# The gathered token tile has its experts picked first, and its rows are asked for while the dense tiles are still being picked

## Chip, cores and metric

The kernel runs on one core of one Trainium2 chip. The metric is device time in microseconds of one execution. TensorE is called PE, VectorE DVE, ScalarE ACT, GpSimd POOL, and SyncE, which issues most of the DMAs, SP.

## What is computed

Two transformer blocks over 512 tokens of width 1024, in f32. The change lies in the second half of the first block, a layer of 16384 small experts. Each token scores 8 heads against two sets of 128 keys, takes the 16 best of each set, then the 16 best of their sums: 128 experts a token, with a softmax gate each.

```python
def peer_sublayer(h, g_ffn, w_peer_q, keys_1, keys_2, peer_u, peer_v):
    x = rmsnorm(h, g_ffn).reshape(-1, shape[-1])
    q = (x @ w_peer_q).reshape(T, PEER_HEADS, PEER_DQ)
    s1 = jnp.einsum('thd,kd->thk', q[..., :half], keys_1).astype(jnp.float32)
    s2 = jnp.einsum('thd,kd->thk', q[..., half:], keys_2).astype(jnp.float32)
    v1, i1 = lax.top_k(s1, PEER_TOPK)
    v2, i2 = lax.top_k(s2, PEER_TOPK)
    cand = (v1[..., :, None] + v2[..., None, :]).reshape(T, PEER_HEADS, PEER_TOPK * PEER_TOPK)
    sc, ci = lax.top_k(cand, PEER_TOPK)
    ...
    act = jax.nn.gelu(jnp.einsum('td,tkd->tk', xt, peer_u[it]), approximate=False)
    return jnp.einsum('tk,tkd->td', gt * act, peer_v[it])
```

## The kernel before

The 512 tokens are four tiles of 128. Tiles 0, 1 and 2 are *dense*: they are multiplied with all 16384 experts, 128 blocks of 128, and a table of gates, zero for experts not picked, keeps what counts. Tile 3 (`GT`) is *gathered*: each token fetches its own 128 rows of `peer_u` and of `peer_v`, in 256 indirect DMAs of 128 rows by 1024 f32 (512 KB), issued by POOL.

**A front** (`front(e)`) loads block e of u (512 KB, by SP), splits it into a high and a low half (`wh` on ACT, `wl` on POOL or, in the loop, on DVE), does 24 matmuls for the dense tiles, and writes the Gelu of the result into a tile `act`. **A product** (`gated_acts`, `products`) loads block e of v, splits it, multiplies `act` by the gates (`gin`, a DMA of 1.5 MB for 8 blocks), splits that into `ah` and `al`, and adds 18 matmuls into six banks `py`.

**Picking.** `topkeys(t)` finds the best keys of tile t on DVE (L914 to L918); `topk(t)` the best sums, and the expert indices through one-hot tiles, compared on DVE (L1051), multiplied on POOL (L1055) and summed on DVE (L1057). For a dense tile indices and gates are transposed into `eT` (L1069); for `GT` they stay in `eg` and `gg`. `spread(t)` makes the gate table of a dense tile in 32 steps: DVE compares (L1080), ACT or POOL scales four one-hots by the gates (L1086, L1083), PE multiplies them, ACT copies the result (L1090), and after four steps SP writes 1 MB to `gates`. `beside(a, na, b, nb)` interleaves two such sequences; each piece calls `step()`, which puts in a front whenever the count of fronts times `PACE` falls behind the steps plus `LEAD`. So 64 of the 128 fronts come before the loop. In this stage a scheduler chooses each engine's order from what is ready.

**The loop** runs over 126 blocks: a product each, and the other 64 fronts spread evenly. POOL and DVE go there in the order of the code. A gather (L960) fills one of four tiles `row`; DVE multiplies it with the token's `xg` and sums (L965, u) or adds it to `yg` (L975, v), two gathers behind the issue. Gathers start at iteration 10 and end at the last. Behind the loop come two last blocks, the sums of each tile and the second transformer block.

**Memory.** The `act` tiles live in two pools, even blocks in one and odd blocks up to `EARLY` in the other. Fronts 42 to 63 (`HOLD` to `AHEAD`) are written to DRAM (`ahead`) and fetched back by `back(e + 5)`.

The functions that the change touches:

Of the kernel before, what the change touches and what calls it, by code (L numbers as in the profile page):

```python
# [26 lines left out]
GT = 3  # L27
# [139 lines left out]
def build(tc, A, OUT):  # L167
# [753 lines left out]
    HOLD, AHEAD = 42, 64  # L921
    ad = dp.tile([AHEAD - HOLD, P, TD], F32, name="ahead")
    EARLY = 84
# [5 lines left out]
    def act_tile(e, side):  # L929
        return (tr if side else tp).tile([P, TD], F32, name="act", bufs=21 if side else 24)  # L930
# [27 lines left out]
    def gather(src, k):  # L958
        r = tg.tile([P, D], F32, name="row", bufs=4)
        G.indirect_dma_start(out=r, out_offset=None, in_=src,  # L960
                             in_offset=bass.IndirectOffsetOnAxis(ap=eg[:, k:k + 1], axis=0))
        return r
# [109 lines left out]
    def spread(t):  # L1072
        NPL = (0, 0, 2)[t]

        t0, eT = t * P, picks[t]
        for b0 in range(0, P, TB):
            stg = tn.tile([P, P, TB], F32, name="stg", bufs=2)
            for q0 in range(0, TB, 4):
                a1 = tn.tile([P, 2, 4, P], F32, name="oh12", bufs=4)
                V.tensor_tensor(a1, iota[:, None, None, :].to_broadcast([P, 2, 4, P]),  # L1080
                                eT[:, :2, b0 + q0:b0 + q0 + 4, None].to_broadcast([P, 2, 4, P]), op=OP.is_equal)
                for q in range(NPL):
                    G.tensor_tensor(a1[:, 1, q], a1[:, 1, q], eT[:, 2, b0 + q0 + q:b0 + q0 + q + 1].to_broadcast([P, P]),  # L1083
                                    op=OP.mult)
                for q in range(NPL, 4):
                    S.activation(a1[:, 1, q], a1[:, 1, q], AF.Copy, scale=eT[:, 2, b0 + q0 + q:b0 + q0 + q + 1])  # L1086
                ps = mmps()
                for q in range(4):
                    TE.matmul(ps[:, q * P:(q + 1) * P], a1[:, 1, q], a1[:, 0, q], start=True, stop=True)  # L1089
                S.copy(stg[:, :, q0:q0 + 4], ps.rearrange("p (q e) -> p e q", q=4))  # L1090
                yield
            nc.sync.dma_start(gd[:, :, (t0 + b0) // TB].rearrange("g p x -> p g x"),
                              stg.rearrange("p (g e) t -> p g (e t)", e=NE))
    order = (0, 1, 2, GT)
    for c in range(2):
        for j in range(2 - 2 * c, 4, 2):
            queries((4 * c + j, 4 * c + j + 1), [w_pq(4 * c + j), w_pq(4 * c + j + 1)])
        for _ in topkeys(0, range(4 * c, 4 * c + 4)):
            pass
# [5 lines left out]
    PACE, LEAD = 3.6, 10  # L1105
    steps = [0]

    def step():

        steps[0] += 1  # L1110
        while len(done_u) < AHEAD and len(done_u) * PACE < steps[0] + LEAD:
            front(len(done_u))
# [12 lines left out]

    beside(topk(0), 23, topkeys(1, range(8)), 16)
    for t in range(3):
        beside(spread(t), 32, chain(topk(t + 1), topkeys(t + 2, range(8)) if t < 2 else iter(())), 39 if t < 2 else 40)
    todo = [("u_rows", g_u, k) for k in range(128)] + [("v_rows", g_v, k) for k in range(128)]
    rows = []  # L1130
    LAG = 2
# [32 lines left out]
    ngather, G0 = len(todo), 10  # L1164
    def use_row():
        f, k, r = rows.pop(0)
        f(k, r)

    with tc.manual_schedule(engines={mybir.EngineType.Pool, mybir.EngineType.DVE}):
        parts, u = gated_acts(0), u_of(AHEAD)  # L1170
        for e in range(P - 2):
# [5 lines left out]
            back(e + 5)  # L1177
# [4 lines left out]
            while len(todo) > max(0, min(ngather, (P - 3 - e) * ngather // (P - 2 - G0))):  # L1182
                src, f, k = todo.pop(0)
                if len(rows) == LAG:
                    use_row()
                if src == "v_rows" and k == 0:
                    while rows:
                        use_row()
                rows.append((f, k, gather(A[src], k)))
# [3 lines left out]
            if e == EARLY + 16:  # L1193
# [440 lines left out]
```

## Time and profile before

| | |
|---|---|
| time, median of 3 runs (lowest, highest) | 2778.35 us (2774.49, 2782.89) |
| the profiled execution: its own time, its span | 2781.33 us, 2779.3 us |
| PE busy | 2621.9 us, 94% |
| DVE busy | 1712.1 us, 62% |
| ACT busy | 1134.9 us, 41% |
| POOL busy | 1039.6 us, 37% |
| DMA, mean over the span | 165 GB/s |

Busy shares are means over stages with different limits. Picking lies between about 625 and 1046 us of the span and the expert loop between 1061 and 1873; what the change is worth is read there.

### The profile page before, as it was taken

The numbers are of one execution on the slowest core, as the hardware profiler recorded it, in microseconds if no ns is written. First come the engines' busy times: TensorE is split into PE (matmuls) and PEld (weight loads), VectorE is DVE, ScalarE is ACT, GpSimd is POOL, SyncE is SP. The second block draws the span as 40 slices with busy tenths as digits, with TensorE's granted clock in tenths as the row PEclk, the third lists the DMA queues.
The fourth block names the chain that finished last, engine by engine and source line by source line (L and its number), as shares of the span: only waits on it lengthen the run. The fifth ranks groups of instructions, "written<-read, shape, count | busy, mean of one in ns | idle before, by whom it ended". The sixth has DMA issues, their size and how long they took to land.

```text
span 2779.3 us, 37248 instructions
## 1 busy us (share of the span) xinstructions
PE 2621.9 (94%) x13809; PEld 2244.2 (81%) x13809; DVE 1712.1 (62%) x3398; ACT 1134.9 (41%) x2064; POOL 1039.6 (37%) x767
## 2 busy tenths in 40 slices
PE   7889999998899898999999999998999999999997
PEld 6768878798899887888888787887666687878886
DVE  5673342248797863788888887896699522533333
ACT  4463342243676553333333333333566432422322
POOL 2322122326546690354455454452333233211111
PEclk9999999999999999999999999998999999999998
DMA  2312213323354566799999889893210133222221
GB/s 100 114 54 78 71 65 125 117 80 101 118 162 150 169 195 238 270 337 360 350 357 345 313 319 339 309 321 136 72 36 24 43 99 98 107 83 99 91 97 55
DMA packets 172485, 458.33 MB, mean 165 GB/s; under 512 B 15248, under 2 KB 73488, under 8 KB 165648
## 3 DMA queue, kind: packets, MB, share of 16 engines
q1 hardware_dynamic: 131984, 316.97, 32.7%
q0 software_dynamic: 36864, 134.23, 14.0%
q10 hardware_dynamic: 3456, 4.76, 0.7%
q8 instruction: 108, 1.77, 0.3%
q14 instruction: 73, 0.60, 0.1%
HBM read 417.43 MB, written 33.69 MB: 162 GB/s over the span
## 4 chain that ended last, share of the span: by engine, by line
PE 60%; DVE 11%; issue 10%; POOL 8%; DMA 3%; ACT 3%; ACTq 0%; SPq 0%; POOLq 0%; DVEq 0%
PE mm L249 33%; PE pu L249 10%; PE py L1161 8%; POOL row L960 4%; PE mm L1089 2%; POOL oh L1055 2%; PE tp L1487 1%; PE o L1492 1%; DVE s L1475 1%; DMA wr<-in_u_T_dram 1%; DVE yg L975 1%; DVE vl L211 1%; POOL wl L211 1%; DVE oh L1080 1%; DMA row<-in_v_rows_dram,eg 1%
## 5 line engine op out<-in xcount | busy, mean ns | idle before, releaser
L211 POOL TENSOR_TENSOR wl<-wr,wh 128x1024 fp32r<-128x1024 f32 (+3 forms) x135 | 325.0, 2408 | 532.8 <-ACT wh L210 237.8
L210 ACT CAST wh<-wr 128x1024 fp32r<-128x1024 f32 (+2 forms) x271 | 274.3, 1012 | 408.3 <-PE mm L249 218.2
L249 PE MATMUL pu<-xf,wh 128*128 128x384 f32 x2048 | 392.2, 343 | 6.8 <-ACT act L947 6.8
L249 PEld LDWEIGHTS pu<-xf,wh 128*128 128x128 f32 x2048 | 362.3, 191 | 13.1 <-ACT act L947 7.8
L960 POOL DMA_INDIRECT row<-in_u_rows_dram,eg x128 | 185.8, 1452 | 263.2 <-DVE row L965 238.6
L960 POOL DMA_INDIRECT row<-in_v_rows_dram,eg x128 | 191.5, 1496 | 190.8 <-DVE yg L975 167.5
L1161 PE MATMUL py<-vh,ah 128*128 128x512 f32 x768 | 202.8, 399 | 29.9 <-ACT ah L210 29.8
L211 DVE TENSOR_TENSOR wl<-wr,wh 128x1024 fp32r<-128x1024 f32 (+2 forms) x136 | 160.5, 1180 | 102.8 <-PE mm L249 61.3
L249 PE MATMUL pu<-xf,wl 128*128 128x384 f32 x1024 | 203.7, 341 | 15.3 <-POOL wl L211 15.3
L1161 PE MATMUL py<-vl,ah 128*128 128x512 f32 x768 | 201.5, 398 | 0.0
L249 PEld LDWEIGHTS pu<-xf,wl 128*128 128x128 f32 x1024 | 183.4, 191 | 18.8 <-POOL wl L211 18.7
L1161 PE MATMUL py<-vh,al 128*128 128x512 f32 x768 | 197.3, 392 | 0.0
L1161 PEld LDWEIGHTS py<-vh,ah 128*128 128x128 f32 x768 | 144.9, 192 | 60.8 <-ACT ah L210 35.8
L210 ACT CAST ah<-act 128x384 fp32r<-128x384 f32 x128 | 65.6, 513 | 312.8 <-DVE act L1151 305.7
L211 DVE TENSOR_TENSOR vl<-vr,vh 128x1024 fp32r<-128x1024 f32 x128 | 156.2, 1221 | 49.3 <-ACT vh L210 49.2
L210 ACT CAST vh<-vr 128x1024 fp32r<-128x1024 f32 x128 | 134.5, 1051 | 125.0 <-PE py L1161 55.8
L1080 DVE TENSOR_TENSOR oh<-iota,eT 128x1024 f32<-128x1024 f32 x96 | 159.5, 1689 | 38.5 <-PE mm L1089 27.3
L975 DVE SCALAR_TENSOR_TENSOR yg<-row,ag,yg 128x1024 f32<-128x1024 f32 x127 | 162.8, 1282 | 19.5 <-DMA row<-in_v_rows_dram,eg 17.5
L1161 PEld LDWEIGHTS py<-vl,ah 128*128 128x128 f32 x768 | 148.4, 193 | 31.9
L1161 PEld LDWEIGHTS py<-vh,al 128*128 128x128 f32 x768 | 145.8, 190 | 30.7
L965 DVE SCALAR_TENSOR_TENSOR row<-row,xg 128x1024 f32<-128x1024 f32 x128 | 152.3, 1220 | 18.8 <-DMA row<-in_u_rows_dram,eg 18.6
L372 DVE TENSOR_TENSOR h<-mm,h 128x512 f32<-128x512 f32 (+1 forms) x54 | 34.1, 632 | 184.9 <-PE mm L249 184.9
(461 smaller groups left out, 5230.6 us busy)
## 6 DMA issues: line engine op xcount, KB each, us to landing
wr<-in_u_T_dram SPq DMA_DIRECT2D x128, 512.0 KB
vr<-in_v_rows_dram SPq DMA_DIRECT2D x128, 512.0 KB
wwr<-in_w_f_dram SPq DMA_DIRECT2D x32, 1024.0 KB
gates<-stg SPq DMA_DIRECT2D x24, 1024.0 KB
gin<-gates SPq DMA_DIRECT2D x16, 1536.0 KB
wr<-in_w_gm_dram SPq DMA_DIRECT2D x16, 512.0 KB
ahead<-act SPq DMA_DIRECT2D x22, 192.0 KB
act<-ahead SPq DMA_DIRECT2D x22, 192.0 KB
```

The costliest lines, as they stand in the source:

```text
L210: S.copy(hi, src)
L211: (lo_eng or V).tensor_tensor(lo, src, hi.bitcast(F32), op=OP.subtract)
L249: TE.matmul(out, w[a][k][:, c0:c0 + P], act[b][k][:, t0:t0 + n], start=i == 0 and k == 0, stop=i == 2 and k == kt - 1)
L372: V.tensor_tensor(h1[k][:, a:b], ps[:, a:b], h1[k][:, a:b], op=OP.add)
L960: G.indirect_dma_start(out=r, out_offset=None, in_=src, in_offset=bass.IndirectOffsetOnAxis(ap=eg[:, k:k + 1], axis=0))
L965: V.scalar_tensor_tensor(r, r, 1.0, xg, op0=OP.mult, op1=OP.mult, accum_out=ag[:, k:k + 1])
L975: V.scalar_tensor_tensor(yg[0], r, ag[:, k:k + 1], yg[0], op0=OP.mult, op1=OP.add)
L1055: G.tensor_tensor(ov[:, h], ov[:, h], iv[:, 4 * c + h, None].to_broadcast([P, 16, 16]), op=OP.mult)
L1080: V.tensor_tensor(a1, iota[:, None, None, :].to_broadcast([P, 2, 4, P]), eT[:, :2, b0 + q0:b0 + q0 + 4, None].to_broadcast([P, 2, 4, P]), ...
L1089: TE.matmul(ps[:, q * P:(q + 1) * P], a1[:, 1, q], a1[:, 0, q], start=True, stop=True)
L1161: TE.matmul(py[2 * t + d], x[:, t * P:(t + 1) * P], w[:, d * 512:(d + 1) * 512], start=e == 0 and i == 0, stop=e == P - 1 and i == 2)
L1475: V.tensor_scalar(s, s, r, None, op0=OP.mult)
```

## The change

`GT` is picked first: `order` begins with it, its `topk` runs beside the keys of tile 0, and a stage of its own (`topk(0)` beside the keys of tile 1) follows. From then on `step()` also issues gathers: one every 6 steps, and one every step while tile 2 is spread. The last stage has nothing beside it. What is left of the gathers (`G1`) is spread over the whole loop, from its first iteration. `row` moves to a pool that lives through both stages and has three tiles in place of four. To make room eight `act` tiles go: `HOLD` is 34, so 30 fronts are spilled and not 22, and `back` runs one block later. POOL no longer scales one-hots in `spread(2)` (`NPL` goes), ACT does all four. `PACE` is 3.5.

```diff
-    HOLD, AHEAD = 42, 64
+    HOLD, AHEAD = 34, 64
...
-    EARLY = 84
+    EARLY = 100
...
-        return (tr if side else tp).tile([P, TD], F32, name="act", bufs=21 if side else 24)
+        return (tr if side else tp).tile([P, TD], F32, name="act", bufs=17 if side else 20)
...
-        r = tg.tile([P, D], F32, name="row", bufs=4)
+        r = tp.tile([P, D], F32, name="row", bufs=3)
...
-                for q in range(NPL):
-                    G.tensor_tensor(a1[:, 1, q], a1[:, 1, q], eT[:, 2, b0 + q0 + q:b0 + q0 + q + 1].to_broadcast([P, P]),
-                                    op=OP.mult)
-                for q in range(NPL, 4):
+                for q in range(4):
                     S.activation(a1[:, 1, q], a1[:, 1, q], AF.Copy, scale=eT[:, 2, b0 + q0 + q:b0 + q0 + q + 1])
...
-    order = (0, 1, 2, GT)
+    order = (GT, 0, 1, 2)
...
-    PACE, LEAD = 3.6, 10
+    PACE, LEAD = 3.5, 10
     steps = [0]
+    todo = [("u_rows", g_u, k) for k in range(128)] + [("v_rows", g_v, k) for k in range(128)]
+    rows = []
+    LAG = 2
+    ngather = len(todo)
...
+    def gather_to(left):
+
+        while len(todo) > left:
+            src, f, k = todo.pop(0)
+            if len(rows) == LAG:
+                use_row()
+            if src == "v_rows" and k == 0:
+                while rows:
+                    use_row()
+            rows.append((f, k, gather(A[src], k)))
+
+    every = [0, 0]
+
     def step():
 
         steps[0] += 1
+        every[1] += 1
+        if every[0] and every[1] % every[0] == 0:
+            gather_to(len(todo) - 1)
...
+    beside(topk(GT), 23, topkeys(0, range(8)), 16)
+    every[0] = 6
     beside(topk(0), 23, topkeys(1, range(8)), 16)
-    for t in range(3):
-        beside(spread(t), 32, chain(topk(t + 1), topkeys(t + 2, range(8)) if t < 2 else iter(())), 39 if t < 2 else 40)
...
+    beside(spread(0), 32, chain(topk(1), topkeys(2, range(8))), 39)
+    beside(spread(1), 32, topk(2), 23)
+    every[0] = 1
+    beside(spread(2), 32, iter(()), 1)
+    G1 = len(todo)
...
-            back(e + 5)
+            back(e + 4)
...
-            while len(todo) > max(0, min(ngather, (P - 3 - e) * ngather // (P - 2 - G0))):
...
+            gather_to(max(0, (P - 3 - e) * G1 // (P - 2)))
```

How it moves instructions, at two places. DVE, before, ahead of the `eT` copy of tile 1: the last index sums of that tile (L1051, L1057) and compares of tile 0's spread (L1080).

```order
L1051 TENSOR_TENSOR oh<-iota,bf 128x1024 x2
L1080 TENSOR_TENSOR oh_6685<-iota,eT 128x1024
L1057 TENSOR_REDUCE ef<-oh 128x64 x2
L1080 TENSOR_TENSOR oh_6736<-iota,eT 128x1024
L1080 TENSOR_TENSOR oh_6788<-iota,eT 128x1024
L1080 TENSOR_TENSOR oh_6801<-iota,eT 128x1024
L1080 TENSOR_TENSOR oh_6865<-iota,eT 128x1024
L1080 TENSOR_TENSOR oh_6916<-iota,eT 128x1024
```

And with the change, the same place and tile (the compare is now L1079; L965 is the product of a gathered row):

```order
L1051 TENSOR_TENSOR oh<-iota,bf 128x1024
L965 SCALAR_TENSOR_TENSOR row,ag<-row,xg 128x1024
L1079 TENSOR_TENSOR oh_7348<-iota,eT 128x1024
L1057 TENSOR_REDUCE ef<-oh 128x64
L965 SCALAR_TENSOR_TENSOR row,ag<-row,xg 128x1024 x3
L1079 TENSOR_TENSOR oh_7370<-iota,eT 128x1024
L1079 TENSOR_TENSOR oh_7416<-iota,eT 128x1024
L965 SCALAR_TENSOR_TENSOR row,ag<-row,xg 128x1024 x2
L1079 TENSOR_TENSOR oh_7480<-iota,eT 128x1024
L965 SCALAR_TENSOR_TENSOR row,ag<-row,xg 128x1024 x3
L1079 TENSOR_TENSOR oh_7501<-iota,eT 128x1024
L1079 TENSOR_TENSOR oh_7553<-iota,eT 128x1024
```

Products of gathered rows now stand between them, up to three in a row: 9 ahead of the first `eT` copy, 12 up to the second, 35 up to the third; behind the third DVE has only compares up to the first `vl` of the loop, 33 of them.

POOL, before, at the end of picking (the low halves of the fronts, the scalings of tile 2, then all gathers):

```order
L211 TENSOR_TENSOR wl<-wr,wh 128x1024
L1083 TENSOR_TENSOR oh_9558<-oh_9558,eT 128x128 x2
L1083 TENSOR_TENSOR oh_9570<-oh_9570,eT 128x128 x2
L1083 TENSOR_TENSOR oh_9584<-oh_9584,eT 128x128 x2
L1083 TENSOR_TENSOR oh_9630<-oh_9630,eT 128x128 x2
L1083 TENSOR_TENSOR oh_9642<-oh_9642,eT 128x128 x2
L1083 TENSOR_TENSOR oh_9654<-oh_9654,eT 128x128 x2
L960 DMA row<-in_u_rows_dram,eg 128x1024 x128
```

And with the change:

```order
L211 TENSOR_TENSOR wl<-wr,wh 128x1024
L960 DMA row<-in_u_rows_dram,eg 128x1024 x3
L211 TENSOR_TENSOR wl<-wr,wh 128x1024
L960 DMA row<-in_u_rows_dram,eg 128x1024 x2
L211 TENSOR_TENSOR wl<-wr,wh 128x1024
L960 DMA row<-in_u_rows_dram,eg 128x1024 x3
L211 TENSOR_TENSOR wl<-wr,wh 128x1024
L960 DMA row<-in_u_rows_dram,eg 128x1024 x3
L211 TENSOR_TENSOR wl<-wr,wh 128x1024 x9
L960 DMA row<-in_u_rows_dram,eg 128x1024 x69
```

59 gathers stand ahead of those of the loop, two or three between one `wl` and the next, and L1083 is gone.

## Rows read from the trace of the kernel before

**Rows 1.** The page's first line.

```profile
span 2779.3 us, 37248 instructions
```

**Rows 2.** Stages: length, busy us of each engine (instructions), granted clock, DMA share, GB/s.

```profile
690.00:1046.00 356.00, 329.23 (x2063) 321.31 (x2062) 274.61 (x654) 228.21 (x531) 224.80 (x164) 0.97 0.52 157
1046.00:1061.50 15.50, 4.54 (x26) 4.22 (x25) 1.78 (x2) 1.55 (x2) 3.84 (x4) 0.76 1.00 366
1160.00:1500.00 340.00, 335.54 (x1614) 295.16 (x1613) 283.72 (x424) 119.86 (x161) 171.37 (x118) 0.99 0.95 348
1500.00:1872.50 372.50, 358.11 (x1703) 314.43 (x1703) 310.15 (x324) 127.72 (x171) 185.41 (x125) 0.98 0.90 322
```

**Rows 3.** DVE's groups, 690 to 1046; then L1080's durations (ns min/median/max).

```profile
L1080 DVE TENSOR_TENSOR oh<-iota,eT 128x1024 f32<-128x1024 f32 x96 | 159.5, 1689 | 38.5 <-PE mm L1089 27.3 <-ACT stg L1090 5.9 <-POOL wl L211 2.6
L1057 DVE TENSOR_REDUCE ef<-oh 128x64 f32<-128x1024 f32 x12 | 14.6, 1220 | 28.7 <-POOL oh L1055 28.7
...
L1080 DVE TENSOR_TENSOR oh<-iota,eT x96: 1196/1235/3424, 694.6 to 1035.4; 128x1024 f32<-128x1024 f32 x96
```

**Rows 4.** POOL's groups, 690 to 1046.

```profile
L211 POOL TENSOR_TENSOR wl<-wr,wh 128x1024 fp32r<-128x1024 f32 x51 | 133.9, 2626 | 102.2 <-ACT wh L210 74.3 <-PE pu L249 16.3 <-PE mm L1089 8.0
L1083 POOL TENSOR_TENSOR oh<-oh,eT 128x128 f32<-128x128 f32 x64 | 45.1, 735 | 5.7 <-DVE oh L1080 5.7
```

**Rows 5.** Timeline of ACT in picking (start, length, count).

```profile
762.36 0.48 ACT L947 ACTIVATE act<-pu 128x384 f32<-128x384 f32 x1
762.75 1.07 ACT L1090 COPY stg<-mm 128x512 f32<-128x512 f32 x2
763.69 2.45 ACT L1086 ACTIVATE oh<-oh,eT 128x128 f32<-128x128 f32 x8
766.04 1.04 ACT L210 CAST wh<-wr 128x1024 fp32r<-128x1024 f32 x1
```

**Rows 6.** Timeline of DVE and of POOL at one place in picking.

```profile
918.59 4.56 DVE L1080 TENSOR_TENSOR oh<-iota,eT 128x1024 f32<-128x1024 f32 x2 [1.24 <-PE mm L1089]
919.40 2.68 POOL L211 TENSOR_TENSOR wl<-wr,wh 128x1024 fp32r<-128x1024 f32 x1 [3.46 <-PE mm L1089]
```

**Rows 7.** DVE's and POOL's groups of the gathered u rows, 1061 to 1873.

```profile
L965 DVE SCALAR_TENSOR_TENSOR row<-row,xg 128x1024 f32<-128x1024 f32 x128 | 152.3, 1220 | 18.8 <-DMA row<-in_u_rows_dram,eg 18.6
L965 DVE DVE_READ_ACCUMULATOR row<-row,xg 128x1 f32 x128 | 10.5, 82 | 0.0
L960 POOL DMA_INDIRECT row<-in_u_rows_dram,eg x124 | 181.8, 1466 | 255.7 <-DVE row L965 238.6 <-issue 17.1
```

**Rows 8.** The chain that ended last, two pieces in the loop; then PE's waits, 1061 to 1873; then the first of them.

```profile
1380.39 4.21 PE pu L249 x24
1384.59 8.16 PE py L1161 x36
...
PE py L1161 <- ACT ah L210: 29.8, 9, 11.0
...
1061.54 2.93 PE L1161 MATMUL py<-vh,ah 128*128 128x512 f32 x6 [11.00 <-ACT ah L210]
```

**Rows 9.** Timeline of SP, ACT, POOL, DVE and PE around one loss in the loop.

```profile
1557.23 0.33 SPq L1148 DMA_DIRECT2D gin<-gates  x1
1563.59 0.44 SPq L222 DMA_DIRECT2D wr<-in_u_T_dram  x1
...
1574.13 1.04 ACT L210 CAST wh<-wr 128x1024 fp32r<-128x1024 f32 x1 [8.69 <-DMA wr<-in_u_T_dram]
...
1556.72 1.30 POOL L960 DMA_INDIRECT row<-in_v_rows_dram,eg  x1 [0.30 <-issue]
...
1568.03 1.28 DVE L975 SCALAR_TENSOR_TENSOR yg<-row,ag,yg 128x1024 f32<-128x1024 f32 x1 [1.98 <-DMA row<-in_v_rows_dram,eg]
...
1576.02 2.93 PE L1161 MATMUL py<-vh,ah 128*128 128x512 f32 x6 [5.50 <-ACT ah L210]
1580.60 1.53 PE L1161 MATMUL py<-vh,al 128*128 128x512 f32 x6
```

**Rows 10.** PE's timeline behind the loop.

```profile
1878.66 1.97 PE L1218 MATMUL pt<-cstt,yg 128*128 128x128 f32 x8 [4.81 <-DVE yg L975]
```

**Rows 11.** SP's waits, 690 to 1046: us in total, times, longest.

```profile
SPq L949 <- ACT act L947: 62.9, 16, 6.1
```

More of the change, by code (lines that the diff above doesn't have):

```diff
@@ L1072, in spread @@
     def spread(t):
-        NPL = (0, 0, 2)[t]
         t0, eT = t * P, picks[t]
@@ L1097, in build @@
             queries((4 * c + j, 4 * c + j + 1), [w_pq(4 * c + j), w_pq(4 * c + j + 1)])
-        for _ in topkeys(0, range(4 * c, 4 * c + 4)):
+        for _ in topkeys(order[0], range(4 * c, 4 * c + 4)):
             pass
@@ L1103, in chain, with use_row @@
             yield from x
-    PACE, LEAD = 3.6, 10
+    PACE, LEAD = 3.5, 10
     steps = [0]
+    todo = [("u_rows", g_u, k) for k in range(128)] + [("v_rows", g_v, k) for k in range(128)]
+    rows = []
+    LAG = 2
+    ngather = len(todo)
+    def use_row():
+        f, k, r = rows.pop(0)
+        f(k, r)
+    def gather_to(left):
[8 more added lines that the diff above has]
+    every = [0, 0]
     def step():
         steps[0] += 1
+        every[1] += 1
+        if every[0] and every[1] % every[0] == 0:
+            gather_to(len(todo) - 1)
         while len(done_u) < AHEAD and len(done_u) * PACE < steps[0] + LEAD:
@@ L1124, in beside @@
             step()
+    beside(topk(GT), 23, topkeys(0, range(8)), 16)
+    every[0] = 6
     beside(topk(0), 23, topkeys(1, range(8)), 16)
-    for t in range(3):
-        beside(spread(t), 32, chain(topk(t + 1), topkeys(t + 2, range(8)) if t < 2 else iter(())), 39 if t < 2 else 40)
-    todo = [("u_rows", g_u, k) for k in range(128)] + [("v_rows", g_v, k) for k in range(128)]
-    rows = []
-    LAG = 2
+    beside(spread(0), 32, chain(topk(1), topkeys(2, range(8))), 39)
[3 more added lines that the diff above has]
+    G1 = len(todo)
     while len(done_u) < AHEAD:
@@ L1162, in products @@
                               start=e == 0 and i == 0, stop=e == P - 1 and i == 2)
[L1164 to L1167, printed above, removed]
     with tc.manual_schedule(engines={mybir.EngineType.Pool, mybir.EngineType.DVE}):
@@ L1181, in build @@
                 u = u_of(len(done_u))
-            while len(todo) > max(0, min(ngather, (P - 3 - e) * ngather // (P - 2 - G0))):
[L1183 to L1189, printed above, removed]
+            gather_to(max(0, (P - 3 - e) * G1 // (P - 2)))
             if not todo:
@@ L1192, in build @@
                     use_row()
-            if e == EARLY + 16:
+            if e == EARLY + 4:
                 str_.close()
```

## Prediction

> **What bounds the kernel now.** I read the page, then the windows by stage, then the groups of each engine in two stages, then the waits and the timeline where PE stood idle. The profiled execution took 2781.33 us around a span of 2779.3 [rows 1], 3 us above the median of the runs shown (2778.35). The sum below is made against 2781.3, and 3 us come off at the end. Two stages are touched.
>
> *Picking*, from 690 us (the first tile of experts is picked) to 1046 (the last gate table leaves). The reader is to see in the windows that no engine is full: of 356 us PE is busy 329, DVE 275, ACT 228, POOL 225 [rows 2]. DVE stands idle 81 us: above all because PE, in its order, has not yet read the one-hot tiles (27.3), and because POOL is still multiplying one-hots for the index sums (28.7) [rows 3].
>
> *The expert loop*, from 1061.5 to 1872.5: 126 products of 18 matmuls and 64 fronts of 24. The chain of waits shows what they cost when nothing is late: 36 matmuls of the product in 8.16, so 4.08 us each, and 4.21 us a front [rows 8]. 126 x 4.08 + 64 x 4.21 = 783.5 us. The loop took 811, so **27.5 us** are lost in it: 18.8 are waits for `ah` after the first one (29.8 less 11.0 [rows 8], and the first lies before 1061.5), the rest slower matmuls behind them. The timeline shows one such loss: a `gin` of 1.5 MB goes out at 1557, the u tile asked for at 1563.59 is cast only at 1574, after 8.69 us of waiting, the cast of `ah` stands behind it on ACT, and PE waits 5.50 us; the six matmuls behind the wait take 2.93 us where six take 1.52 otherwise, PE at the lower of its two levels (1.2 and 2.4 GHz) [rows 9]. DMA is busy 95% and 90% of the two long windows [rows 2]. So the loop is PE's, with DMA as what disturbs it.
>
> **The change part by part.** *In the loop.* The order shows 59 gathers issued before the loop, so 197 remain: 1.56 an iteration in place of 2.03. Bytes an iteration, before: v 512 KB, 64/126 u tiles 260, `gin` 192, rows 1040, spilled activations 34, in all 2038 KB in 6.44 us, 324 GB/s, which agrees with 348 and 322 [rows 2]. After: rows 801, spills 46, in all 1811 KB; in 6.3 us that is 294 GB/s, 16% below what the window of 348 carried. The queue then drains between two `gin`. I take 20 of the 27.5 us back. Bounds: 25 (only the slow start after 1061.5 remains) and 8 (the bursts still hit a u tile). DVE has 57 rows less there, but PE doesn't wait for DVE's share, so that is worth nothing more. At the end PE waits 4.81 us for the last gathered rows [rows 10]; with fewer rows an iteration I take 3 of it (0 to 5). Three row buffers in place of four: a row is used every 4.0 us, so 12 us lie between release and use, against 11.5 before; no cost.
>
> *In the picking stage, DVE.* 57 products of a row with `xg` come in before the loop. One takes 1.22 us plus 0.08 for the read of its sum [rows 7], so 74 us. That price is from a stage in which POOL only issues gathers. In the picking stage POOL also makes the low halves `wl`, and there DVE's instructions on two tiles are slower: L1080 has a median of 1.235 and a mean of 1.689 [rows 3, 6]. The timeline shows why: of two L1080 from 918.59 that take 4.56 us, the second ends one L1080 after POOL's `wl` has ended [rows 6]. The product reads two tiles too. With the same 0.45 us each it is 57 x 0.45 = 26 us more, so 74 to 100, and I take 88. So DVE is to be busy about 275 + 88 = 363 us, where the whole stage took 356.
>
> The Trainium skill, SBUF — State Buffer, section "Who interferes with whom", says that a DVE instruction with two SBUF inputs contends with a GpSimd instruction that reads SBUF, and that the first one holds the ports for its whole length. The 918.59 row agrees; by that rule the upper end would hold, DVE at 375 and the sum 12 us above mine, by the loop's row alone the lower, 349 and 14 us below mine.
>
> DVE can't be full all the time either. The order shows that the scheduler pulls 56 of the 57 products ahead of the last tile's `eT` copy; behind it DVE has 33 one-hot compares and little else. That last stretch goes at ACT's pace, since the change gives ACT all four scalings of a step: eight of them take 2.45 us and two copies 1.07 [rows 5], so a step is 4 x 0.306 + 0.53 = 1.75 us; 37 steps 65 us, and 8 fronts with a cast and a Gelu at 1.25 to 1.5 us about 10: 75 us. DVE's part of it is 33 x 1.45 = 48, so 27 us of DVE are idle there. Of the 28.7 us in which DVE waited for POOL's products about half are covered by gathered rows that the order sets there; 14 stay. The waits for PE go, since DVE is now behind. So 363 + 27 + 14 = 404 us in place of 356: I take **+44** after some 4 us for POOL, which gives up L1083. Bounds: 349 + 15 + 5 = 369, **+13** (no contention, holes filled); 375 + 27 + 14 + 10 = 426, **+70**.
>
> *POOL.* It loses L1083, 45.1 us, and gains 59 gathers at 1.47 us [rows 4, 7], 87. 225 + 42 = 267 of some 400: not the bound. But a gather waits for its row buffer, and behind it in POOL's queue stands the `wl` of the next front, for which PE waits. *ACT* gains 64 scalings at 0.306, 20 us, on 228 of 356: hidden up to the last stretch, counted there. *PE* has the same work, 329 us in now 400; its idle time there costs clock, but PE is not what the stage waits for. *SP*: eight more spilled tiles (30 for 22) are 16 issues, each in front of a u load; 16 waits of such writes took 62.9 us of SP's time [rows 11], so 8 more may take 31, under the cover of a PE that DVE holds up; bare it would be 10 at most, as u loads have two buffers. The first stage before 690 and the step from 1046 to 1061.5 (v tile, `gin` after the last table) stay as they are [rows 2]. Side of the pools, `back(e + 4)` and the new spill bound move only waits with more than 20 us of slack.
>
> Sum: +44 - 20 - 3 = **+21**: 2802 for the profiled execution, 2799 against the median.
>
> **The rivals.** *Faster: the rows fit into DVE's holes.* 74 us of products against 81 idle. For it: the holes are there, and the order puts rows just where DVE waits for POOL. Against it: 27 us of holes are waits for a PE that is 92% busy, and the last stretch can't use rows that are already done. It holds if the products stay at 1.30 us and the last stretch falls under 60 us: picking 0 to +8, loop and end -23, so about -18: 2763, 2760 against the median. Below +13 in the picking stage the change is measurably faster. Chance 0.26.
>
> *Even.* Picking +15 to +30, eaten up by the loop: 2778 against the median. 0.18.
>
> *Slower by more: the row buffers.* In the order rows stand in threes with two compares between; three buffers are then to be refilled in 3 x 1.7 + 2 x 1.7 - 1.7 = 6.8 us, with 1.47 us of POOL, a `wl` of 2.6 perhaps ahead of it [rows 4], and the landing. How long a row takes to land in a DMA queue half empty no row shows: more than 1.5 us (512 KB at the 348 GB/s of the loop), less than the 11.3 of the row that is issued at 1556.72 and used at 1568.03 [rows 9]. At 5 us a triple stalls DVE 1.5 to 2 us, and 19 triples give +28 to +38: about 2830. 0.16. The Trainium skill, DMA: Bandwidth & Descriptors, section "Anatomy of one DMA", gives 2.0 us plus bytes at 436 GB/s, 3.2 us as an estimate for a row, by which this stall would be near zero; no run here shows it alone.
>
> *Slower: no relief in the loop.* The `gin` bursts alone cause the losses; the loop gives 5, the sum is +36: 2814. 0.12.
>
> That the gathers aren't early at all is excluded by the order.
>
> **How the numbers follow.** My case (2787 to 2815, likeliest 2799) has 0.28. Measurable is 0.3%, 8.3 us. Faster: 0.26; within: 0.18; slower: 0.28 + 0.16 + 0.12 = 0.56. The range from 2764 (below it a tenth: all the holes filled, loop at its floor) to 2832 (above it a tenth: triples stalling at their full price). My case alone would have 2787 to 2815.
>
> **What would show it.** Right: first product of the loop near 1105 instead of 1061.5; DVE 90% busy from 690 on, L965 there at 1.4 to 1.7 us; last stretch behind the third `eT` of 70 to 80 us; waits of `py` for `ah` in the loop under 10 us besides the first, DMA at 80 to 85%; loop near 790. Wrong: a first product before 1075 (DVE's holes took the rows); L965 at 1.22 (no contention); losses in the loop every 50 us as before; DVE waiting for `row` over 20 us (the buffers).

## The result, and the profile after

The changed kernel takes **2813.58 us** (2813.0 to 2817.46, 4 runs) against 2778.33 (2774.49 to 2782.89, 4 runs) run beside it: a ratio of 1.0122 [1.0104, 1.0141], 35 us slower. The profiled execution took 2813.35 us, its span is 2811.6, 32.3 more than [rows 1].

The windows of the changed kernel (length, busy us of PE, PEld, DVE, ACT and POOL with counts, granted clock, DMA share, GB/s): the picking stage, its parts before and behind the last `eT`, and two of the loop.

```profile
690.00:1117.00 427.00, 358.19 (x2071) 344.88 (x2070) 335.65 (x763) 241.99 (x593) 259.48 (x156) 0.92 0.67 206
690.00:1038.80 348.80, 283.46 (x1561) 271.98 (x1560) 293.93 (x729) 171.36 (x401) 238.69 (x149) 0.90 0.65 205
1038.80:1117.00 78.20, 74.73 (x513) 72.90 (x512) 41.72 (x34) 70.63 (x194) 20.78 (x8) 1.00 0.72 212
1140.00:1500.00 360.00, 359.37 (x1740) 317.75 (x1739) 271.48 (x369) 133.51 (x178) 131.89 (x93) 1.00 0.87 312
1500.00:1840.00 340.00, 340.00 (x1654) 301.72 (x1654) 259.65 (x279) 123.97 (x165) 125.16 (x86) 1.00 0.82 292
```

Against [rows 2]: picking takes 427 us in place of 356. DVE is busy 61 us more (335.7 for 274.6), and its idle time didn't shrink: 91 us for 81. In the loop PE is now busy all the time, with DMA at 82 to 87%.

DVE's groups from 690 to 1130 that changed or wait (busy us and mean ns; behind the second bar the idle time before them and what ended it):

```profile
L1079 DVE TENSOR_TENSOR oh<-iota,eT 128x1024 f32<-128x1024 f32 x96 | 138.9, 1480 | 30.2 <-PE mm L1085 30.2
L965 DVE SCALAR_TENSOR_TENSOR row<-row,xg 128x1024 f32<-128x1024 f32 x56 | 88.1, 1590 | 36.7 <-DMA row<-in_u_rows_dram,eg 36.7
L1057 DVE TENSOR_REDUCE ef<-oh 128x64 f32<-128x1024 f32 x12 | 14.6, 1219 | 20.4 <-POOL oh L1055 20.4
```

A row's product costs 1.59 us here, 1.22 in the loop [rows 7]; the compares are cheaper than in [rows 3] (1.48 for 1.69). New is the middle line's idle time: 36.7 us in which DVE stands before a product because its row has not landed. All DVE's waits from 690 to the last `eT` copy at 1038.8 are two lines (us in total, times, longest):

```profile
DVE row L965 <- DMA row<-in_u_rows_dram,eg: 36.7, 15, 5.6
DVE ef L1057 <- POOL oh L1055: 20.4, 11, 4.3
```

So up to there DVE sets the pace: 293.9 us busy and 57 of these waits make up the 349 us of the second window to within 2 us. It waits for PE only behind, 30.2 us. The timeline of POOL and DVE shows a place where DVE waits for rows (start, length, in brackets the idle time before; gathers, `wl` and the products they bear on):

```profile
815.73 0.98 POOL L960 DMA_INDIRECT row<-in_u_rows_dram,eg  x1 [0.15 <-issue]
...
818.25 1.68 POOL L960 DMA_INDIRECT row<-in_u_rows_dram,eg  x1 [1.53 <-DVE row L965]
819.95 2.35 POOL L211 TENSOR_TENSOR wl<-wr,wh 128x1024 fp32r<-128x1024 f32 x1
821.29 2.10 DVE L965 SCALAR_TENSOR_TENSOR row<-row,xg 128x1024 f32<-128x1024 f32 x1 [2.17 <-DMA row<-in_u_rows_dram,eg]
822.45 1.77 POOL L960 DMA_INDIRECT row<-in_u_rows_dram,eg  x1 [0.16 <-issue]
...
825.59 1.22 DVE L965 SCALAR_TENSOR_TENSOR row<-row,xg 128x1024 f32<-128x1024 f32 x1
...
828.04 2.39 POOL L211 TENSOR_TENSOR wl<-wr,wh 128x1024 fp32r<-128x1024 f32 x1
828.68 2.85 DVE L965 SCALAR_TENSOR_TENSOR row<-row,xg 128x1024 f32<-128x1024 f32 x1 [1.86 <-DMA row<-in_u_rows_dram,eg]
```

Rows are used in the order in which they are asked for: the one of 815.73 is used at 821.29, that of 818.25 at 825.59 without a wait, that of 822.45 at 828.68. Where DVE stood waiting, a row was there 5.6 and 6.2 us after its gather began, and with three buffers the gather itself waits for a product (818.25: 1.53 us behind L965). The two products that begin beside a `wl` take 2.10 and 2.85 us and end 1.1 us after that `wl`; the one that has none beside it takes 1.22.

The waits of DVE and PE in the loop, from 1140 to 1840:

```profile
DVE vl L211 <- ACT vh L210: 78.1, 51, 3.1
...
PE py L1183 <- ACT ah L210: 0.6, 1, 0.6
```

PE's timeline behind the loop, and its matmuls of `vh` and `ah` with the start of the first and of the last:

```profile
1912.61 1.07 PE L1228 MATMUL pt<-cstt,yg 128*128 128x128 f32 x8 [1.45 <-DVE yg L975]
```

```profile
L1183 PE MATMUL py<-vh,ah x768: 387/389/794, 1130.2 to 1922.2; 128*128 128x512 f32 x192
```

PE waits for `ah` 0.6 us there, where behind the first wait it lost 18.8 [rows 8], and for `yg` 1.45 in place of 4.81 [rows 10]. By stage: the first product comes at 1130.2 instead of 1061.5 [rows 8], **+68.7**; from it to the last product's start are 792.0 us, where the kernel before takes 827.5 (1061.5 to 1889.0), **-35.5**; behind it -0.9. Together 32.3.

### The profile page after: what moved, and what is told of

It is laid out like the page before. It is cut to its first block, busy times and chain, and to the rows that moved or that the text cites. A ratio compares the mean times of both kernels' runs of the same rounds, so it can differ in the third digit from the quotient of the medians.

```text
span 2811.6 us, 37261 instructions
## 1 busy us (share of the span) xinstructions
PE 2632.4 (94%) x13809; PEld 2256.9 (80%) x13809; DVE 1713.7 (61%) x3398; ACT 1151.3 (41%) x2128; POOL 984.6 (35%) x703
## 4 chain that ended last, share of the span: by engine, by line
PE 69%; DVE 12%; POOL 4%; ACT 4%; DMA 4%; issue 2%; ACTq 0%; SPq 0%; DVEq 0%; POOLq 0%
PE mm L249 33%; PE py L1183 18%; PE pu L249 11%; DVE oh L1079 2%; POOL oh L1055 2%; DMA row<-in_u_rows_dram,eg 2%; DVE row L965 1%; PE tp L1497 1%; PE o L1502 1%; DVE s L1485 1%; POOL wl L211 1%; ACT oh L1082 1%; DMA gates<-stg 1%; DVE s L1459 1%; PE s L682 1%
## 5 line engine op out<-in xcount | busy, mean ns | idle before, releaser
L249 PE MATMUL pu<-xf,wh 128*128 128x384 f32 x2048 | 400.2, 348 | 11.0 <-ACT act L947 8.2
L249 PEld LDWEIGHTS pu<-xf,wh 128*128 128x128 f32 x2048 | 370.8, 195 | 18.5 <-ACT act L947 10.2
L249 PEld LDWEIGHTS pu<-xf,wl 128*128 128x128 f32 x1024 | 184.9, 193 | 35.4 <-POOL wl L211 35.2
L965 DVE SCALAR_TENSOR_TENSOR row<-row,xg 128x1024 f32<-128x1024 f32 x128 | 174.2, 1382 | 47.0 <-DMA row<-in_u_rows_dram,eg 47.0
L1082 ACT ACTIVATE oh<-oh,eT 128x128 f32<-128x128 f32 x384 | 123.1, 403 | 133.1 <-DVE oh L1079 133.0
L1079 DVE TENSOR_TENSOR oh<-iota,eT 128x1024 f32<-128x1024 f32 x96 | 138.9, 1480 | 30.2 <-PE mm L1085 30.2
```

The lines of the kernel that those rows point to most:

```text
L249: TE.matmul(out, w[a][k][:, c0:c0 + P], act[b][k][:, t0:t0 + n], start=i == 0 and k == 0, stop=i == 2 and k == kt - 1)
L965: V.scalar_tensor_tensor(r, r, 1.0, xg, op0=OP.mult, op1=OP.mult, accum_out=ag[:, k:k + 1])
```

## The experiments

All of them in one table. "First" is the start of the loop's first matmul of `vh` and `ah`, "loop" the time from it to the start of the last one; ratios are to the kernel before, timed beside each (2778.3 to 2783.2).

| kernel | median us | ratio [95%] | first | loop |
|---|---|---|---|---|
| before | 2778.33 | | 1061.5 | 827.5 |
| after | 2813.58 | 1.0122 [1.0104, 1.0141] | 1130.2 | 792.0 |
| e1 no early gathers, 3 buffers | 2807.39 | 1.0090 [1.0062, 1.0117] | 1059.5 | 853.8 |
| e5 no early gathers, 4 buffers | 2746.05 | 0.9876 [0.9853, 0.9899] | 1059.7 | 794.2 |
| e6 no early gathers, 6 buffers | 2744.10 | 0.9873 [0.9849, 0.9898] | 1059.4 | 791.2 |
| e9 before, gathers from iteration 0 | 2747.10 | 0.9873 [0.9852, 0.9894] | 1059.2 | 793.9 |
| e12 before, short products | 2747.40 | 0.9879 [0.9863, 0.9896] | 1065.1 | 791.2 |
| e8 before, gate tables in parts | 2765.95 | 0.9949 [0.9934, 0.9964] | 1060.5 | 813.1 |
| e2 after, 4 buffers | 2802.38 | 1.0073 [1.0050, 1.0096] | 1120.4 | 791.6 |
| e10 after, short early products | 2790.26 | 1.0025 [1.0012, 1.0039] | 1106.7 | 791.8 |
| e3 after, no early products | 2774.91 | 0.9967 [0.9950, 0.9983] | 1088.3 | 791.5 |
| e7 as e3, early rows of 64 KB | 2787.39 | 1.0026 [1.0013, 1.0039] | 1100.6 | 791.9 |
| e4 after, early products on a resident tile | 2800.97 | 1.0070 [1.0048, 1.0091] | 1113.6 | 791.8 |
| e11 as e6, POOL scales too | 2750.25 | 0.9885 [0.9864, 0.9907] | 1063.4 | 794.0 |

My theory was that of the prediction: the products fill DVE in the picking stage, and fewer bytes an iteration let the loop run free. The rivals were the row buffers, POOL's queue and the new order itself for the first stage; DVE's time and the bursts of gate tables for the second.

**e1: the order alone.** The early gathers are left out; the gathered tile is still first, and all 256 gathers start at iteration 0.

```diff
     beside(topk(GT), 23, topkeys(0, range(8)), 16)
-    every[0] = 6
...
-    every[0] = 1
     beside(spread(2), 32, iter(()), 1)
```

> Gathered tile first, all 256 gathers in the loop from iteration 0. If the early rows' work on DVE (products and waits, 61 us more busy time) is what made the picking stage 71 us longer: first product of the loop near 1065 to 1075 instead of 1130, and the loop loses about 30 us again as in the kernel before; in all 2778 to 2795. If the new order itself costs (a last stretch at ACT's pace with nothing of DVE beside it): first product at 1095 or later, and with the loop's loss back the time is 2805 or more. If the loop was helped by the order and not by fewer rows: loss in the loop under 10 us.

The first product comes at 1059.5, 2 us before that of the kernel before: the order, the spills and ACT's four scalings, which this kernel keeps, cost nothing, and the 70.7 us between this and the changed kernel are all the early rows'. But the kernel is slow: its loop takes 853.8 us, 26 more than before. I had expected the old loss, not twice as much. From 1140 to 1840 DVE stands 86.8 us before products whose rows are not there (35.2 in the kernel before), and PE 36.6 for `ah`.

**e5, e6: as e1, with four and six row buffers.** The buffers stand in the loop's own pool, as before the change; with six, four rows are asked for ahead in place of two.

```diff
-        r = tp.tile([P, D], F32, name="row", bufs=3)
+        r = tg.tile([P, D], F32, name="row", bufs=4)
```

> Gathered tile first, all 256 gathers in the loop from iteration 0, four row buffers as in the kernel before. With three buffers the same kernel lost some 64 us in the loop and DVE waited 99 us there for rows. If the third buffer's short turn is the cause: waits for rows near 36 us as before the change, 1060 us to the first product, the time 2775 to 2785. If 2.03 rows in every iteration from the first are too many whatever the buffers (traffic), or the other parts of the edit (more spills, a later release of the side pool): the time stays at 2795 or more.

> As the one with four row buffers and no early gathers, but six buffers and a row used four gathers later. If rows' landing time is what is left of the loop's loss (DVE late with the gates because it waits for a row): waits for rows under 10 us, loop loss under 20, the time 2760 to 2772. If u tiles held up by bursts of gate tables are: loop loss stays at 28 to 35 and the time at 2775 to 2785.

A fourth buffer is worth 61 us there: 2746, faster than both kernels and than I had expected in any case. The loop takes 794 us, with **all 256 rows in it**; with six buffers 791.2, which only e12 equals, and the kernel is 2 us faster still, within the intervals. So the loop's loss was not in the number of rows that it fetches in all. (e5 changes the pool and the count of the buffers at once; e9 below has the old pool and agrees.) That a loop with 30% more rows than the changed kernel's runs as smoothly contradicts the prediction's reason for its gain.

**e9: the kernel before, one constant.**

```diff
-    ngather, G0 = len(todo), 10
+    ngather, G0 = len(todo), 0
```

> The kernel before with one constant changed: G0 from 10 to 0, so that its gathers are spread over all 126 iterations (2.03 each) and not over the last 116 (2.2 each). If the rate alone is what the loop could not carry: the loss in the loop falls from 33 us to under 8 and the time to 2745 to 2752, as in the kernel with the new order and four buffers. If the order or the spill and pool numbers made that loop smooth: the time stays at 2770 to 2786.

2747.1. The 256 gathers over 126 iterations, 2.03 each, in place of 116 with 2.2 each, take away the loss that the kernel before has. Neither the new order nor the spill and pool numbers have a part in it: e5 and e9 agree within their intervals.

**e12: the kernel before, short products.** At 2.2 rows an iteration, each product covers an eighth of its row.

```diff
-        V.scalar_tensor_tensor(r, r, 1.0, xg, op0=OP.mult, op1=OP.mult, accum_out=ag[:, k:k + 1])
+        V.scalar_tensor_tensor(r[:, :P], r[:, :P], 1.0, xg[:, :P], op0=OP.mult, op1=OP.mult, accum_out=ag[:, k:k + 1])
...
-            V.scalar_tensor_tensor(yg[0], r, ag[:, k:k + 1], yg[0], op0=OP.mult, op1=OP.add)
+            V.scalar_tensor_tensor(yg[0][:, :P], r[:, :P], ag[:, k:k + 1], yg[0][:, :P], op0=OP.mult, op1=OP.add)
```

> The kernel before (2.2 rows an iteration after the tenth), in which every product of a row covers 128 of its 1024 columns (the gathered tile's output is then wrong): the same rows are fetched, DVE's time for each falls from 1.3 us to about 0.65. If the bytes of the rows are what the loop could not carry at 2.2 an iteration (they come to 345 GB/s at PE's pace, and 347 is the most that a window carried): PE still loses 20 us or more in the loop, the time 2765 to 2782. If DVE's time for the rows is (gated activations stand behind three products in some iterations): the loss is gone, the time 2743 to 2752.

The loss is gone with every byte still fetched. Its windows in the loop:

```profile
1140.00:1500.00 360.00, 359.93 (x1750) 318.86 (x1749) 193.68 (x459) 130.33 (x176) 136.81 (x128) 1.00 0.96 355
1500.00:1840.00 340.00, 340.00 (x1651) 301.44 (x1650) 193.34 (x316) 122.88 (x166) 128.87 (x121) 1.00 0.94 344
```

DMA is at 96% and 355 GB/s, more than in [rows 2], and PE never stands. A short product also frees its buffer earlier, but rows that land late are not what is gone: from 1140 to 1840 DVE waits 44.9 us for rows here, 35.2 in the kernel before. It is DVE that had no time to spare. Its timeline in the kernel before shows it (the rows of `wl` and of the products, and one of `al`):

```profile
1533.46 1.22 DVE L211 TENSOR_TENSOR wl<-wr,wh 128x1024 fp32r<-128x1024 f32 x1
1534.60 2.60 DVE L975 SCALAR_TENSOR_TENSOR yg<-row,ag,yg 128x1024 f32<-128x1024 f32 x2
...
1539.44 0.56 DVE L211 TENSOR_TENSOR al<-act,ah 128x384 fp32r<-128x384 f32 x1 [0.64 <-ACT ah L210]
1539.92 2.60 DVE L975 SCALAR_TENSOR_TENSOR yg<-row,ag,yg 128x1024 f32<-128x1024 f32 x2
...
1545.24 1.22 DVE L211 TENSOR_TENSOR wl<-wr,wh 128x1024 fp32r<-128x1024 f32 x1
1546.37 2.60 DVE L975 SCALAR_TENSOR_TENSOR yg<-row,ag,yg 128x1024 f32<-128x1024 f32 x2
...
1551.68 3.92 DVE L975 SCALAR_TENSOR_TENSOR yg<-row,ag,yg 128x1024 f32<-128x1024 f32 x3
...
1558.32 1.22 DVE L211 TENSOR_TENSOR wl<-wr,wh 128x1024 fp32r<-128x1024 f32 x1
```

From one `wl` to the next are two iterations and one front. PE takes 8.16 + 4.21 = 12.37 us for them [rows 8]. DVE takes 11.78 with two rows and two (1533.46 to 1545.24), 13.08 with two and three; in both figures are two waits of 0.64 us, in which ACT makes `ah` out of DVE's `act` before DVE can go on with `al`. At 2.2 rows an iteration that is 11.78 + 0.41 x 1.30 = 12.32 on average: 0.05 us to spare in 12.37, so next to nothing that comes late, a row or a gate table, is made up. At 2.03 it is 11.86, half a us to spare, at 1.56 some 10.6.

These are rounds with v rows, which are used from 1497.84 on. With u rows DVE is quicker, 11.29 us for two and two:

```profile
1387.78 1.22 DVE L211 TENSOR_TENSOR wl<-wr,wh 128x1024 fp32r<-128x1024 f32 x1
...
1399.07 1.22 DVE L211 TENSOR_TENSOR wl<-wr,wh 128x1024 fp32r<-128x1024 f32 x1
```

With a fifth it is some 1.2 us more, so about 11.8 at 2.2 rows an iteration and 0.6 to spare. The waits of PE for `ah` in the kernel before go with that: 4.4 of the 18.8 us lie before 1497.84 and 14.4 behind. Why 4.4 are left where DVE has 0.6 us is not shown.

What DVE has to spare can also be read from one line of its waits: DVE waits for `vh`, which ACT makes when PE has freed its buffer, only where DVE is ahead. From 1140 to 1840, in the kernel before and then in e9:

```profile
DVE vl L211 <- ACT vh L210: 3.5, 5, 1.1
```

```profile
DVE vl L211 <- ACT vh L210: 20.3, 30, 2.0
```

In the changed kernel it was 78.1, with a loop no more than 2 us shorter than that of e9 (792.0 and 793.9).

**e8: the kernel before, gate tables in four parts**, each fetched in every second iteration of the group before.

```diff
-        if e % NE == 0:
-            gated_acts.g = tg.tile([P, NTB, NE * TB], F32, name="gin", bufs=2)
-            nc.sync.dma_start(gated_acts.g, gd[e // NE])
+        if e % NE == 0:
+            gated_acts.g = gated_acts.n
+        if e % 2 and e // NE + 1 < P // NE:
+            q = e % NE // 2
+            if q == 0:
+                gated_acts.n = tg.tile([P, NTB, NE * TB], F32, name="gin", bufs=2)
+            nc.sync.dma_start(gated_acts.n[:, 6 * q:6 * q + 6], gd[e // NE + 1, :, 6 * q:6 * q + 6])
```

> The kernel before with each 1.5 MB gate table of the loop fetched in four parts, one every second iteration of the group before, so that no single 1.5 MB transfer stands ahead of a u tile. If the bursts cause the loop's loss (33 us over the floor, 18.8 of waits for ah): waits for ah under 6 us besides the first, the time 2750 to 2765. If the total of bytes does (2038 KB an iteration): same time within 8 us, 2770 to 2786.

2766: 14 of the 36 us. The bursts of [rows 9] are one of the things that come late; a DVE with time to spare makes up for all of them (e9 fetches its tables whole), and without it breaking up the burst helps in part. Waits for `ah` stayed at 11.5, above the 6 that I had named.

**e2: the changed kernel with a fourth row buffer.** Two more activations are spilled for the room (32 for 30).

```diff
-    HOLD, AHEAD = 34, 64
+    HOLD, AHEAD = 32, 64
...
-        return (tr if side else tp).tile([P, TD], F32, name="act", bufs=17 if side else 20)
+        return (tr if side else tp).tile([P, TD], F32, name="act", bufs=16 if side else 19)
...
-        r = tp.tile([P, D], F32, name="row", bufs=3)
+        r = tp.tile([P, D], F32, name="row", bufs=4)
```

> A fourth row buffer (room from four more spilled activations... HOLD 34 to 32, so 32 spills for 30). If the landing of rows into three buffers is what the stage waits for: DVE's waits for a row fall from 36.7 us to under 15, the picking stage is 20 to 30 us shorter, the time near 2785 to 2793. If DVE's load (or ACT's pace at the end) sets the stage: its waits move elsewhere, the first product comes at most 8 us earlier, the time 2805 to 2815.

Between the two: DVE's waits for rows fall from 36.7 to 22.2, the first product comes 9.8 us earlier. The waits are on the path, as the two lines of the result say; what a buffer more takes off them comes back to about two thirds.

**e10: the changed kernel with short early products.** As in e12, for the first 57 only, so that waits and releases of the rows stay.

```diff
+    V.memset(ag, 0.0)
+
     def g_u(k, r):
+        if k < 57:
+            V.scalar_tensor_tensor(r[:, :P], r[:, :P], 1.0, xg[:, :P], op0=OP.mult, op1=OP.mult,
+                                   accum_out=ag[:, k:k + 1])
+            return
```

> The changed kernel, in which the first 57 u products cover 128 of the 1024 columns (the gate sums are then wrong), so DVE's load falls by some 80 us, while each product still waits for its row and still frees its buffer, so that gathers go out as before. If DVE's load makes the picking stage long: first product at 1065 to 1080, the time 2750 to 2765. If the waits for rows or the rows' traffic do: first product at 1105 or later, the time 2785 or more.

DVE's groups from 690 to the first product:

```profile
L1085 DVE TENSOR_TENSOR oh<-iota,eT 128x1024 f32<-128x1024 f32 x96 | 140.8, 1505 | 29.2 <-PE mm L1091 29.2
L968 DVE SCALAR_TENSOR_TENSOR row<-row,xg 128x128 f32<-128x128 f32 x56 | 36.1, 655 | 60.0 <-DMA row<-in_u_rows_dram,eg 59.9
```

The products take 52 us less, the first product comes 23.5 us earlier, and the waits for rows grow from 36.7 to 59.9. So less than half of the picking stage's loss is the products' length. Where DVE has the time, it spends it before a row that hasn't landed: 5.6 to 6.2 us a row, three buffers, and DVE's compares queued behind in its order.

**e3, e7: no early products at all**, with the 57 gathers whole, and with 64 KB each. The first edit is in both, the second in e7 alone.

```diff
+    V.memset(ag, 0.0)
+
     def g_u(k, r):
+        if k < 57:
+            return
```

```diff
-        G.indirect_dma_start(out=r, out_offset=None, in_=src,
+        w = P if short and k < 57 else D
+        G.indirect_dma_start(out=r[:, :w], out_offset=None, in_=src.rearrange("e (a w) -> (e a) w", w=w),
```

> The first 57 u products are left out (their gate sums stay zero), the 57 rows are still fetched. If DVE's part (88 us of products and 37 us of waits for rows) makes the stage long: first product at 1060 to 1075, the loop as in the changed kernel, the time 2745 to 2760. If POOL (gathers in front of the low halves) or DMA traffic make it long: first product at 1100 or later, the time 2785 or more.

> The first 57 u products are left out, as in the run without products (first product 1088.3, 29 us later than without any early gather), and the 57 early gathers fetch 64 KB each in place of 512 KB (wrong rows, unused). Same number of gather instructions on POOL. If the bytes delay the u tiles (68 us of ACT waiting for u tiles in that run): first product at 1060 to 1068, those waits near 29 us, the time 2748 to 2755. If POOL's issuing (81 us of its time ahead of the low halves) costs: first product at 1080 or later, the time as without products, 2770 to 2775.

e3's first product comes 42 us earlier than the changed kernel's but still 29 behind e1's, between the two cases that I had named. e7 was to divide these 29 between bytes and POOL, and came out the other way from what the theory of bytes expects: with an eighth of the bytes it is 12 us later than e3. Without products nothing holds the gathers back, and the order puts most of them in the first 100 us. Of e7 from 690 to 790 the window, two groups of POOL, and SP's wait in front of a u tile:

```profile
690.00:790.00 100.00, 64.36 (x270) 59.94 (x269) 47.11 (x227) 17.21 (x23) 84.93 (x76) 0.78 0.28 85
```

```profile
L961 POOL DMA_INDIRECT row<-in_u_rows_dram,eg x50 | 49.4, 989 | 15.0 <-issue 12.7 <-DMA row<-in_u_rows_dram,eg 2.3
L211 POOL TENSOR_TENSOR wl<-wr,wh 128x1024 fp32r<-128x1024 f32 x10 | 23.6, 2362 | 0.2
```

```profile
SPq L222 <- POOL wl L211: 97.4, 10, 13.5
```

DMA is 28% busy, yet ACT waits for u tiles: SP can ask for the next only when POOL's `wl` has read the last, and between two `wl` stand five or six gathers. Fifty gathers take 49 + 15 us of POOL, and PE is busy 64 us of 100. So gathers cost by their place in POOL's queue when they come in bunches. In the changed kernel the products space them out, and PE's waits for `wl` are near those of e1 (23.2 us from 690 to 1130, against 20.1 to its first product), so this is a cost of e3 and e7, not of the change, and e3 can't serve to price the rows' traffic.

**e4: the early products on a resident tile**, so that they never wait for a row; two more activations are spilled, as in e2.

```diff
...
+    res = tp.tile([P, D], F32, name="res")
...
     def g_u(k, r):
+        if k < 57:
+            V.scalar_tensor_tensor(res, xg, 1.0, xg, op0=OP.mult, op1=OP.mult, accum_out=ag[:, k:k + 1])
+            return
```

> The first 57 u products read a tile that is resident (the token tile twice) and write a tile of their own, so they cost DVE the same but never wait for a row; the rows are fetched and not used (32 spills for 30). If DVE's load sets the stage: products at 1.45 to 1.65 us, the first product within 12 us of 1130, the time 2800 to 2815. If the waits for rows do (36.7 us): first product at 1090 to 1100, the time 2775 to 2785.

Inconclusive: with no row to wait for, 33 of the 57 products were put ahead of 690, where they delay the picking itself (first `eT` copy at 782.3, 760.2 in the changed kernel). It does not separate load from waits; e10 and e2 do.

**e11: POOL does two of four scalings again** in the last spread tile, in the kernel of e6.

```diff
+        NPL = (0, 0, 2)[t]
...
-                for q in range(4):
+                for q in range(NPL):
+                    G.tensor_tensor(a1[:, 1, q], a1[:, 1, q], eT[:, 2, b0 + q0 + q:b0 + q0 + q + 1].to_broadcast([P, P]),
+                                    op=OP.mult)
+                for q in range(NPL, 4):
                     S.activation(a1[:, 1, q], a1[:, 1, q], AF.Copy, scale=eT[:, 2, b0 + q0 + q:b0 + q0 + q + 1])
```

> The kernel without early gathers and with six row buffers, in which POOL again does two of the four scalings of a step in the last spread tile, as before the change. In that stretch (968 to 1035) ACT is busy 94% and PE 98%. If the stretch goes at ACT's pace: it takes 45 to 55 us instead of 66, the time 2729 to 2736. If PE's work (fronts and spreads) sets it: no change, 2740 to 2748.

The last stretch of e6 and then that of e11:

```profile
968.40:1034.90 66.50, 65.06 (x460) 64.42 (x460) 48.81 (x34) 62.61 (x171) 19.64 (x7) 1.00 0.72 209
```

```profile
968.20:1038.90 70.70, 65.92 (x457) 63.84 (x455) 51.56 (x34) 49.23 (x116) 64.64 (x64) 1.00 0.70 203
```

ACT falls from 62.6 to 49.2 us, and the stretch doesn't get shorter but 4 us longer, with POOL at 64.6. POOL may hold it up in turn (PE waits 4.6 us for its one-hots), so e11 alone doesn't say what set the pace in e6. The first of the two windows does: PE is busy 65.06 of 66.5 us there, so a faster ACT could have given 1.4 us at most. The stretch is PE's.

## Why the prediction was right, and where not

**The sign and the range were right**, 2813.6 inside 2764 to 2832 with slower at 0.56; the likeliest time, 2799, was 15 too low. Its two large terms were both mis-sized, by 27 and by 10 us, in opposite directions, and the loop's term stood on a wrong cause: that the sum came within 15 us is in part luck. A sign that the prediction had named against itself came true, DVE waiting over 20 us for `row` (36.7), and one for it did not, DVE 90% busy from 690 on (84% up to the last `eT` copy).

**Picking: +44 predicted, +71 measured**, just outside the upper bound of 70.
- *L965 at 1.4 to 1.7 us there*: 1.59. Right, and for the reason given: beside POOL's `wl` an instruction on two tiles is slower. The Trainium skill, SBUF — State Buffer, section "Who interferes with whom", has this contention; the trace agrees (1.59 against 1.22 in the loop, two products that end 1.1 us after the `wl` beside them, and in e10 and e12 0.655 against 0.287 for a product of 128 columns).
- *DVE busy +88*: it was +61. The products came to 88.1 + 4.4 us as computed; the compares fell by 20.6 us, which I had held constant, and the rest by some 11, in many short instructions and in overlaps. These 27 us less than forecast would by themselves have made the stage shorter than the sum.
- *The waits for PE go, since DVE is now behind*: right up to the last `eT` copy, where none is left.
- *14 us of holes before POOL's products stay*: 20.4.
- *No term for rows that land late into three buffers*: **the step that failed**. 36.7 us of waits for rows stand on DVE's path, and the sum had none. The prediction's "no cost" for the buffers is worked out for the loop, and there it holds (DVE waits 13.5 us for rows from 1140 to 1840, PE 0.6 for `ah`); it left picking out. There late rows were a rival of their own with 0.16, priced at 28 to 38 us from a landing of 5 us; the landing was 5.6 to 6.2. The mechanism belonged into the sum. In a loop with 2.03 rows an iteration the missing buffer is worth 61 us (e1 against e5). By the figures of the Trainium skill, DMA: Bandwidth & Descriptors, section "Anatomy of one DMA", a row is 3.2 us, an estimate; the timeline shows nearly twice that, from the start of the issue, with other transfers under way.
- *The last stretch at ACT's pace, 75 us with 27 of DVE idle*: 78.2 with 36.5. The number was good, its cause wrong: PE is busy 74.7 of the 78.2 us, and the 3.5 that are left are its waits for ACT, the most that a faster ACT could give. In the kernel without early gathers it is the same (e6, e11).

Together: 27 us less of busy time, 36.7 of waits for rows, 6 before POOL's products and 9.5 in the last stretch more come to +25 on the 404 of the sum, 429 against 427 measured.

**Loop: -20 predicted (bounds -8 to -25), -30 measured**, from 811 to 781 us. There was more to gain than the 27.5 us of the prediction. It counted 64 whole fronts in the loop, but the matmuls with the high halves of two of them run ahead of the first product:

```profile
1044.69 5.84 PE L249 MATMUL pu<-xf,wh 128*128 128x384 f32 x32
```

So 783.5 is some 5.7 us too high and the loss was 33. The step "the queue then drains between two `gin`" named bytes, and "DVE has 57 rows less there, but PE doesn't wait for DVE's share, so that is worth nothing more" was wrong: with all bytes but short products (e12) the loss is gone, and with the full products too once no more than 2.03 come in an iteration (e9). The trace of before had the evidence: ACT's `ah` behind DVE's `act`, and groups of three products in DVE's timeline. I read the one loss at 1557, which a late u tile caused, and took its cause for that of all. Since at 2.03 nothing is left to gain (794 against 792 in the changed kernel), moving 59 rows out bought only what spreading them from iteration 0 gives without any cost.

**End: -3 predicted, -5 measured**: the first wait for `yg` is 1.45 for 4.81, and the matmuls behind it are quicker, eight of `pt` in 1.07 for 1.97. The step from the last table to the first product, which was to stay, is 2 us shorter (13.2 for 15.5).

The rivals: *rows fit into the holes* fell with DVE's idle time, 91 us for 81; *no relief in the loop* fell with 792 against 827; *even* needed picking at half its loss.

**What stays open.** How the 71 us of picking divide exactly: shortening the products gives back 23.5, one buffer 9.8, and the two overlap, since waits grow when products shrink; more than four buffers there were not tried. Nor was the kernel before at 2.2 rows with more than four buffers, which would tell how much of its loss is DVE's time and how much rows that land late behind it.

**The version that beats both** is the kernel without early gathers and with six buffers, 2744.1; the kernel before with `G0` at 0 does the same within the intervals, by a single constant.

## What to carry to other kernels

Add up each engine's time for one round of a loop, start to start from the timeline, and compare it with the bound engine's round: an in-order engine with 0.05 us to spare in 12.4 looks 83% busy in a window (579 of 700 us from 1140 on, in the kernel before), since its round has waits for another engine in it, and yet can't make up for what is late. Before work is moved out of a loop, try to spread it evenly inside. And work that is put into the holes of an in-order engine brings its own waits along: a product whose row takes 6 us to land holds up everything queued behind it, so the busy share alone doesn't tell whether a hole can be filled; the buffers count too.

## What the runs showed of the hardware

- DMA at 96% and 355 GB/s (e12) did not hold up PE, which was busy 359.9 of the 360 us; a share near full is no bound by itself.
- A gather of 512 KB landed 5.6 to 6.2 us after its issue began, in a stretch where DMA was 65% busy.
- A product of two tiles that begins beside a `wl` of POOL ends 1.1 us after that `wl` has ended (821.29 and 828.68 above: 2.10 and 2.85 us in place of 1.22).
- A gather's issue takes POOL up to twice as long when DVE works on two tiles at that moment. In the changed kernel from 690 to 1040 the 19 issues without such an instruction beside them took 0.94 to 0.99 us, the 38 others 1.67 on average and 1.96 at most. The timeline of e7 on DVE and POOL, where DVE makes no product of rows:

```profile
759.30 1.22 DVE L1062 TENSOR_REDUCE ef<-oh 128x64 f32<-128x1024 f32 x1 [1.98 <-POOL oh L1060]
759.42 0.98 POOL L961 DMA_INDIRECT row<-in_u_rows_dram,eg  x1 [0.16 <-issue]
...
760.64 1.21 DVE L1056 TENSOR_TENSOR oh<-iota,bf 128x1024 f32<-128x1024 f32 x1
760.71 1.96 POOL L961 DMA_INDIRECT row<-in_u_rows_dram,eg  x1 [0.30 <-issue]
```

  Beside a reduction of one tile 0.98 us, beside a compare of two, begun just ahead of it, 1.96. Fifty such issues took 0.99 on average there; in the loop of the kernel before, with a product or a split beside most of them, 1.47 [rows 7].
- PE's granted clock was 0.90 from 690 to 1038.8, where it stood idle for 65 us of 349, and 0.97 in [rows 2], with 27 of 356; in the last stretches above, where it stood 1.4 to 4.8 us, it was 1.00, the upper of its two levels (1.2 and 2.4 GHz).
